# Another order of small constants and two paddings in SBUF under a two-layer float32r encoder kernel

## Chip, cores and metric

One NeuronCore of one Trainium2 chip runs the whole program. The metric is the device time of one execution in microseconds. Of the kernel before, three runs are shown: 2837.61, 2838.25 and 2838.52 us, median 2838.25 us.

## What is computed

Two encoder layers over 1024 tokens of 1024 channels, all in float32. Each layer is a token mixer, a SwiGLU FFN and a gated embedding, each with a norm ahead and a residual behind:

```python
for i in range(2):
    hn = rms_norm(h, norm_mix[i])
    mix = gla_mixer(hn, ...) if i == 0 else diff_attn_mixer(hn, ...)
    h = h + mix
    h = h + swiglu(rms_norm(h, norm_ffn[i]), ffn_w_in[i], ffn_w_out[i])   # hidden width 2816
    gate = sigmoid(rms_norm(h, ple_norm[i]) @ ple_w_gate[i])
    h = h + gate * (p[i] @ ple_w_proj[i])
```

The first mixer is a bidirectional gated linear attention of 4 heads, the second a differential softmax attention of 8 heads.

## The kernel before

**Products.** Every large product is split into high and low float32r parts and taken as three matmuls (`mm3`, L146 to L150). The first operand is the stationary one (loaded as weights), the second is streamed:

```python
def mm3(ps, lhs, rhs, start, stop):
    (lh, ll), (rh, rl) = lhs, rhs
    nc.tensor.matmul(ps, lh, rl, start=start, stop=False)   # L148
    nc.tensor.matmul(ps, ll, rh, start=False, stop=False)   # L149
    nc.tensor.matmul(ps, lh, rh, start=False, stop=stop)    # L150
```

So each matmul has its own weight load (LDWEIGHTS), and the weights of the next one are loaded while this one streams.

**Stages, in order of time.** GLA: projections in pieces of a few matmuls (`trans_proj`, `tok_proj`) strewn among the steps of the recurrence (`sps`, `ups`, `ops`, `kups`), then its output projection (`out_tiles`, names `go`). FFN of layer 0: input projection by Strassen-Winograd products (`prod`, L923; names `f_0ps` to `f_21ps`; 22 units of 7 products of 12 matmuls with 512 columns), then the output projection (`out_step`, L1017; `f0o`). The embedding's gate (`Ple.gate`, L1162; `pl`). The differential attention: values (`Values.blocks`, `dv`), then a pipeline of projections (`pmm`, `dp`), scores (`qkt`, `da..s`), transposes (`T`, `da..tp`; `tkm`, `dp..tk`) and value products (`AV`, `da..av`), its output projection (`do`); FFN and gate of layer 1 (`f1o`). The order on TensorE, VectorE, ScalarE and GpSimd is written out by hand and is not touched.

**Where tiles lie.** Pools opened on the left are stacked upward in SBUF in the order in which they are opened: `const`, `praw`, `pw`, `ph`, `tiny` (L80 to L84), then the stage's own pool (`gla`, `fx0`, `diff`, ...). Pools on the right (`hxg`, `hxd0`) are stacked downward from the top. Within a pool, tiles stand in the order in which their tags first appear; each is rounded up to 32 bytes a partition. The first free byte on the left is 16512, which is 128 modulo 512; the top is 480 modulo 512. Nearly all large tiles are multiples of 512 bytes, so a whole pool has one residue, shifted by the small tiles that stand before it:

| tiles (address modulo 512) | before |
|---|---|
| `ident`, `identr` (operands of transposes) | 128 |
| `praw`, `pw`, `ph`: FFN input weights, transposed tiles of `go`, `do` and gates, projection weights and values of the attention | 384 |
| left stage pools: FFN operands `T` 1, 2, 7, 6, gate weights, `kst`, `dq`, half of `hxd` | 256 |
| GLA's tiles behind `mid` (`qk`, `ku`, `vv`, `s`, `p`) | 128 |
| right pools: `hxg`, the other half of `hxd`, FFN operands `T` 5, 3, 4, output weights of layer 0 | 480 |

The pairs (streamed, weights) that follow: FFN input products (256, 384) and (480, 384), in both layers; `f0o` (480, 480) behind its first 48 matmuls, which have (384, 384); `f1o` in turns of 48 matmuls (256, 480) and (480, 480); `go` (480, 384); `do` half (480, 384) and half (256, 384); gates (256, 384); `dv` and `dp` (384, 480) and (384, 256); `AV` (256, 384); scores (256, 256); `ups`, `ops`, `sps` (128, 128).

Of the kernel before, what the change touches and what calls it, by code (L numbers as in the profile page):

```python
# [9 lines left out]
F32 = mybir.dt.float32  # L10
# [8 lines left out]
P = 128  # L19
# [15 lines left out]
PACE, PACE_END = 0.67, 0.72    # microseconds of projections among a step's stages  # L35
# [7 lines left out]
# what precedes the recurrence of the first mixer, in the order in which it is emitted  # L43
# [21 lines left out]
def kernel(  # L65
# [22 lines left out]

    ident = const.tile([P, P], F32, name="ident")
# [3 lines left out]
    mhalf = const.tile([P, 8], F32, name="mhalf")  # L93
# [34 lines left out]
    def block_t(pool, name, bufs=2):  # L128
        """16 KB: four rows of 1024."""
        return pool.tile([P, 4, D], F32R, tag="x", name=name, bufs=bufs)  # L130

    def load_wout(w, pools, bufs, name, engs, lead=1):
        """Output weights, k by k, in blocks that held the projections' operand."""
        wo, raw = [], {}
        for k in range(-1, KT):
            for i in range(0 if k < 0 else k + lead, min(k + lead + 1, KT)):
                raw[i] = rawt(f"{name}{i}_raw")
                nc.sync.dma_start(raw[i], w[sl(i), :])
            if k >= 0:
                if k % 4 == 0:  # L140
                    blk = [block_t(pools[k // 4], f"{name}{k}{z}", bufs) for z in range(2)]
                wo.append(both(blk, ALL, k % 4))
                hi_lo(raw.pop(k), *wo[k], engs[k % len(engs)])
            yield wo
# [53 lines left out]
    def load_p(layer, i, raw):  # L198
        """256 tokens of the embedding, channels on partitions."""
        nc.sync.dma_start(raw, p[layer, 0][:, sl(i, 256)].rearrange("(k p) t -> p k t", p=P))  # L200
# [12 lines left out]
    # ---------------------------------------------------------------- GLA  # L213
    def gla(hx, hx_pool, gain):
        """The mixer; returns the residual tiles, a per-tile generator and its pool."""
# [7 lines left out]
        # The gates' projections have 32 channels z between them. The first takes the weights' high parts three  # L223
        # times and the low parts side by side, so that two passes do (the fourth group of rows has the product
        # with the low parts); the second takes all its products in one pass, with the rows
        # (high, low, high, rest) of z over the rows (high, high, low, high) of its weights.
        wg = pool.tile([P, 2, 512], F32R, name="wg")
        bg = const.tile([P, 2, GH], F32, name="bg")
# [24 lines left out]
        rs = const.tile([P, GH, NT], F32, name="rs")  # L253
# [4 lines left out]
        # --- projections: generators that yield after every few products  # L258
        class W:
            """One weight block, loaded and split in parts of 4 KB."""  # L260
# [28 lines left out]
        def trans_proj(w, dst, key, nm):  # L289
            """Channels on partitions: [128, 1024]."""  # L290
            t = ht(nm + "T", [2, 512])
            dst[key] = t.rearrange("p a b -> p (a b)")
            ps = ptA(nm + "ps")
            for half in range(2):
                for k in range(KT):
                    mm3(ps[:, half, :], w.at(k), hx_k(hx, k, half), k == 0, k == KT - 1)
                    yield 0.65
            yield 0.0
            nc.scalar.copy(t, ps)

        def tok_proj(w, emit, nm):
            """Tokens on partitions: per token tile [128, 256]."""
# [13 lines left out]
        def ple_proj(w, nm):  # L316
            """The embeddings' projection, for later."""
# [51 lines left out]
        def jobs(names):  # L369
            """A chain of projections; the next weights are loaded and split one ahead."""  # L370
# [8 lines left out]
            for j, (n, h) in enumerate(names):  # L379
# [9 lines left out]
                if nxt:  # L389
                    nxt.load()  # L390
                    todo = list(nxt.parts())
                    # parts that must wait for this block's slots are split after it
                    free = 6 - 2 * len(list(w.parts())) if n + nxt.name[1] != "rp" else 4
                    early, todo = todo[:free // 2], todo[free // 2:]
                else:
                    early = []
# [18 lines left out]
        # --- log-gate sums of (head, direction): inclusive running sums, over a token tile (from its  # L415
        # far end for the backward direction), of TAU times the log gates; channels on partitions
# [25 lines left out]
        def gc(h, d, half):  # L442
            if (h, d) not in gate:
                gate[h, d] = (ht(f"B{h}_{d}"), pool.tile([P, 3, NT], F32, tag="mid", name=f"mid{h}_{d}", bufs=4))
# [19 lines left out]
        # --- the recurrence, by steps (head, direction, tile)  # L464
# [155 lines left out]
        # --- the first head's operands, by halves of the tokens  # L620
# [85 lines left out]
        # The steady state is a pipeline of one step; (stage, offset) in the order in which a step emits them.  # L706
        # F is a share of the projections; the gates of a head take the steps of the head before.
# [26 lines left out]
        # the output weights take the place of the projections' operand, half by half  # L734
# [49 lines left out]
    mid = {}    # what goes between the halves of an output tile  # L784

    def out_tiles(hs, h_dram, wo, load, comp, nm):
        """h += source @ wo, by token tiles; yields the tile that is done (or a negative number) and, between, None."""
# [29 lines left out]
    # ---------------------------------------------------------------- FFN  # L817
    # The input projection is taken in Winograd's form of Strassen's product: per pair of blocks of 128
    # channels (rows of A = W^T), K halves and token halves (columns of B; even and odd token tiles),
    # seven products in place of eight.  # L820
    #   products: 1 = A11 B11, 2 = A12 B21, 3 = S4 B22, 4 = A22 T4, 5 = S1 T1, 6 = S2 T2, 7 = S3 T3
    #   S1 = A21 + A22, S2 = S1 - A11, S3 = A11 - A21, S4 = A12 - S2
    #   T1 = B12 - B11, T2 = B22 - T1, T3 = B22 - B12, T4 = B21 - T2
    #   C11 = 1 + 2, C12 = 1 + 6 + 5 + 3, C21 = 1 + 6 + 7 + 4, C22 = 1 + 6 + 5 + 7
    def ffn(layer, hs, tiles, g, hx_pools, bufs, next_pool, early):
        """From the mixer's tiles on; returns the tiles of h after the FFN."""
# [9 lines left out]
        # --- operand B: norm, sums (in place, tokens on partitions), transposes  # L836
# [28 lines left out]
        def put_x(t):  # L865
            """Transposes of a tile; its halves, then what the sums make of them, are kept in its place."""
# [22 lines left out]
        # --- operand A: unit u has the channel blocks 2 (u // 2) and the next, of the gate or the up half  # L889
# [32 lines left out]
        # --- products and what they go into  # L922
# [7 lines left out]
        def evac(u, p):  # L930
# [5 lines left out]
            if u < 2 and p == 2:  # L936
                # here the second product comes before the sixth, which still needs the first
# [22 lines left out]
        # --- the order of the products on the tensor engine; for the first two units around the last transposes  # L960
# [9 lines left out]
        def prepare(n):  # L970
            """All that comes before the split of product n."""
# [13 lines left out]
        # --- the output projection, by halves of the tokens (four tiles) with all of K on chip  # L985
# [54 lines left out]
        with tc.manual_schedule(engines={E.PE, E.DVE, E.Activation, E.Pool}):  # L1040
            at = {"mul": 0, "put": 0}

            def advance(t, n):
                """What goes before output tile t (n = -1) and after its halves."""
# [28 lines left out]
            for z in seq:  # L1073
# [6 lines left out]
                else:  # L1080
# [9 lines left out]
                    # the second product is added when the first is no longer wanted  # L1090
                    # from the third unit on, the second product waits for the sixth
# [25 lines left out]
    # ---------------------------------------------------------------- per-layer embedding  # L1117
# [18 lines left out]
    class Ple:  # L1136
        """The gate and its sum into the residual, by token tiles; the next layer's norm follows where there is one."""
# [50 lines left out]
    # ---------------------------------------------------------------- differential attention  # L1188
    class Values:
        """Values of all heads, by blocks of 256 channels."""  # L1190
# [39 lines left out]
    def diff(hx, hx_pools, h_dram, val, between):  # L1230
# [12 lines left out]
        ls = const.tile([P, 2], F32, name="ls")  # L1243
        neglam = const.tile([P, 1], F32, name="neglam")
# [31 lines left out]
        # query and key weights of one head  # L1276
# [19 lines left out]
        # The steady state is a pipeline of period two query tiles. An attention step takes the  # L1296
        # query tile i of all heads, a projection step the token tile u, a value step the pair m.
# [50 lines left out]
        # the query tiles 2 m and 2 m + 1 together, channels on partitions  # L1348
# [133 lines left out]
        # (stage, offset) in the order in which a period emits them; pairs count in periods  # L1482
# [17 lines left out]
        def piece():  # L1500
            """A part of the values' projection; with it the weights of the first heads."""
# [44 lines left out]
        def ple_proj():  # L1546
            """The second layer's embeddings' projection, half a tile at a time."""
# [66 lines left out]
    # ---------------------------------------------------------------- the trunk  # L1614
# [97 lines left out]
_LAYOUT = {'p': (0, 1, 3, 2)}    # channels before tokens  # L1712
# [40 lines left out]
```

## Time and profile before

| | |
|---|---|
| median of 3 runs | 2838.25 us |
| profiled execution, span | 2836.8 us |
| TensorE busy | 2774.1 us, 98% of the span, 15272 matmuls |
| VectorE, ScalarE, GpSimd busy | 55%, 46%, 42% |
| bytes moved by DMA | 283.59 MB, mean 100 GB/s |
| granted TensorE clock, mean | 0.998 |

The page gives the span alone for the profiled execution; the median lies 1.4 us above it. A matmul's duration in the trace overlaps that of the next one, so durations do not add up; what adds up is the spacing from one matmul's start to the next one's.

### The profile page before, as it was taken

What the parts mean: (1) busy time and instruction counts of PE and PEld (TensorE: products, weight loads), DVE (VectorE), ACT (ScalarE), POOL (GpSimd) and SP (SyncE); (2) the same over time, 40 slices, a digit from 0 to 9 for tenths busy, and PEclk for the clock granted to TensorE, in tenths of its full rate; (3) what the DMA queues carried; (4) which work ended last, traced back from release to release, by engine and by line L of the source; (5) the groups of instructions that cost most, each with busy time, mean ns of one, the idle gap of its engine ahead of it and who ended that gap; (6) DMA issues with size and microseconds to landing.
All of it is one profiled execution on the core that took longest, in us unless ns stands there. A gap on an engine that the chain in (4) does not pass through costs nothing.

```text
span 2836.8 us, 40481 instructions
## 1 busy us (share of the span) xinstructions
PE 2774.1 (98%) x15272; PEld 2368.8 (84%) x15272; DVE 1565.1 (55%) x2390; ACT 1297.5 (46%) x2723; POOL 1203.4 (42%) x1364
## 2 busy tenths in 40 slices
PE   8999999999999999999999999989999999999999
PEld 7899988788888888889989999878878888888887
DVE  5677775644444434354169898884564444444333
ACT  5776673433322332233368788784342322342222
POOL 3233331455555420010588888872165555530000
PEclk9999999999999999999999999999999999999999
DMA  4121265122222564333211111135222222374422
GB/s 123 40 64 60 79 223 174 67 83 89 82 67 89 196 205 141 97 99 109 74 53 42 38 42 38 34 119 197 75 76 81 89 76 74 114 258 138 146 68 80
DMA packets 199955, 283.59 MB, mean 100 GB/s; under 512 B 14544, under 2 KB 158928, under 8 KB 199760
## 3 DMA queue, kind: packets, MB, share of 16 engines
q1 hardware_dynamic: 199760, 281.00, 30.7%
q8 instruction: 121, 1.98, 0.3%
q14 instruction: 74, 0.61, 0.1%
HBM read 215.95 MB, written 65.01 MB: 99 GB/s over the span
## 4 chain that ended last, share of the span: by engine, by line
PE 81%; DVE 8%; POOL 5%; ACT 3%; issue 2%; DMA 1%; SPq 0%; POOLq 0%; DVEq 0%; ACTq 0%
PE f1o L148 3%; PE f1o L150 3%; PE f1o L149 3%; PE f0o L148 3%; PE f0o L149 3%; PE f0o L150 3%; PE dp L148 1%; PE dp L150 1%; PE dp L149 1%; PE dv L148 1%; PE dv L150 1%; PE dv L149 1%; PE do L148 1%; PE do L149 1%; PE do L150 1%
## 5 line engine op out<-in xcount | busy, mean ns | idle before, releaser
L148 PE MATMUL dp<-dw,hxd 128*128 128x256 f32 x512 | 148.5, 290 | 2.0 <-DVE da5dt L1345 0.3
L150 PE MATMUL dp<-dw,hxd 128*128 128x256 f32 x512 | 144.1, 281 | 0.0
L149 PE MATMUL dp<-dw,hxd 128*128 128x256 f32 x512 | 143.9, 281 | 0.0
L148 PE MATMUL f1o<-f1W,f1A 128*128 128x512 f32 x336 | 132.2, 393 | 0.0
L150 PE MATMUL f1o<-f1W,f1A 128*128 128x512 f32 x336 | 131.9, 393 | 0.0
L149 PE MATMUL f1o<-f1W,f1A 128*128 128x512 f32 x336 | 131.7, 392 | 0.0
L148 PE MATMUL f0o<-f0W,f0A 128*128 128x512 f32 x336 | 130.8, 389 | 0.0
L150 PE MATMUL f0o<-f0W,f0A 128*128 128x512 f32 x336 | 130.7, 389 | 0.0
L149 PE MATMUL f0o<-f0W,f0A 128*128 128x512 f32 x336 | 130.7, 389 | 0.0
L148 PEld LDWEIGHTS dp<-dw,hxd 128*128 128x128 f32 x512 | 96.6, 189 | 3.5 <-DVE da5dt L1345 0.6
L149 PEld LDWEIGHTS dp<-dw,hxd 128*128 128x128 f32 x512 | 96.7, 189 | 0.1
L150 PEld LDWEIGHTS dp<-dw,hxd 128*128 128x128 f32 x512 | 96.5, 189 | 0.0
L150 PEld LDWEIGHTS f1o<-f1W,f1A 128*128 128x128 f32 x336 | 63.0, 188 | 14.6
L149 PEld LDWEIGHTS f1o<-f1W,f1A 128*128 128x128 f32 x336 | 63.0, 188 | 14.3
L148 PEld LDWEIGHTS f1o<-f1W,f1A 128*128 128x128 f32 x336 | 63.0, 188 | 14.3
L150 PEld LDWEIGHTS f0o<-f0W,f0A 128*128 128x128 f32 x336 | 63.1, 188 | 13.2
L148 PEld LDWEIGHTS f0o<-f0W,f0A 128*128 128x128 f32 x336 | 63.1, 188 | 13.1
L149 PEld LDWEIGHTS f0o<-f0W,f0A 128*128 128x128 f32 x336 | 63.1, 188 | 12.9
L148 PE MATMUL dv<-dwv,hxd 128*128 128x256 f32 x256 | 72.6, 284 | 0.0
L149 PE MATMUL dv<-dwv,hxd 128*128 128x256 f32 x256 | 71.9, 281 | 0.0
L150 PE MATMUL dv<-dwv,hxd 128*128 128x256 f32 x256 | 71.9, 281 | 0.0
L154 POOL TENSOR_SCALAR pn10r<-pn10ss 128x1 f32<-128x1 f32 x1 | 0.2, 191 | 169.1 <-ACT pn10xn L1146 169.1
(4446 smaller groups left out, 10022.0 us busy)
## 6 DMA issues: line engine op xcount, KB each, us to landing
pw_raw<-in_ple_w_gate_dram SPq DMA_DIRECT2D x16, 512.0 KB, 6.1
dqk_raw<-in_diff_w_in_dram SPq DMA_DIRECT2D x32, 256.0 KB, 3.9
x<-in_x_dram SPq DMA_DIRECT2D x8, 512.0 KB, 5.9
wv_raw<-in_gla_w_in_dram SPq DMA_DIRECT2D x8, 512.0 KB, 3.8
wr_raw<-in_gla_w_in_dram SPq DMA_DIRECT2D x8, 512.0 KB, 3.8
o_dram<-o SPq DMA_DIRECT2D x32, 128.0 KB, 1.9
r_dram<-r SPq DMA_DIRECT2D x16, 256.0 KB, 2.2
gwo_raw<-in_gla_w_out_dram SPq DMA_DIRECT2D x8, 512.0 KB, 3.7
```

The lines of the kernel that those rows point to most:

```text
L148: nc.tensor.matmul(ps, lh, rl, start=start, stop=False)
L149: nc.tensor.matmul(ps, ll, rh, start=False, stop=False)
L150: nc.tensor.matmul(ps, lh, rh, start=False, stop=stop)
L154: nc.gpsimd.tensor_scalar(r, ss, scale, EPS, ALU.mult, ALU.add)
```

## The change

Five small tiles of `const` (`mhalf`, `bg`, `rs`, `ls`, `neglam`) are allocated ahead of `ident`, with a padding of 96 bytes behind them, and `tiny` gets a padding of four buffers of 32 bytes. The tile `mid` grows from three rows to four (96 to 128 bytes a partition). Comments and docstrings are dropped too, which moves line numbers by up to four.

```diff
@@ tile_encoder_kernel, behind the pools
+    mhalf = const.tile([P, 8], F32, name="mhalf")
+    bg = const.tile([P, 2, GH], F32, name="bg")
+    rs = const.tile([P, GH, NT], F32, name="rs")
+    ls = const.tile([P, 2], F32, name="ls")
+    neglam = const.tile([P, 1], F32, name="neglam")
+    const.tile([P, 24], F32, name="pad0")
+    tiny.tile([P, 8], F32, tag="pad", name="pad1")
     ident = const.tile([P, P], F32, name="ident")
...
-    mhalf = const.tile([P, 8], F32, name="mhalf")
     nc.vector.memset(mhalf, -0.5)
@@ gla
-        bg = const.tile([P, 2, GH], F32, name="bg")
...
-        rs = const.tile([P, GH, NT], F32, name="rs")
...
-                gate[h, d] = (ht(f"B{h}_{d}"), pool.tile([P, 3, NT], F32, tag="mid", name=f"mid{h}_{d}", bufs=4))
+                gate[h, d] = (ht(f"B{h}_{d}"), pool.tile([P, 4, NT], F32, tag="mid", name=f"mid{h}_{d}", bufs=4))
@@ diff
-        ls = const.tile([P, 2], F32, name="ls")
-        neglam = const.tile([P, 1], F32, name="neglam")
```

The small tiles take 32 + 32 + 128 + 32 + 32 + 96 = 352 bytes, so `ident` starts at 16512 + 352 = 16864, which is 480 modulo 512; `identr` (512 bytes) and the 4 KB tile of the gains follow, and `praw` starts at 480 too. With the padding `tiny` ends at 480, and with four buffers of 128 bytes for `mid` all of GLA's later tiles do. Of the 15272 matmuls, 15144 then have (480, 480); the other 128 are transposes of keys in the attention, (480, 224). Before, 1584 matmuls of the FFN output projections have equal residues (`f0o` and half of `f1o`), and some 1200 short ones: the scores and GLA's small products.

The order of instructions is the same on every engine, and so are all waits; the only instructions that differ are the readers and writers of `mid`, whose row of 24 elements becomes one of 32.

## Rows read from the trace of the kernel before

**Rows 1.** The page: its head and the busy time of each engine.
```profile
span 2836.8 us, 40481 instructions
PE 2774.1 (98%) x15272; PEld 2368.8 (84%) x15272; DVE 1565.1 (55%) x2390; ACT 1297.5 (46%) x2723; POOL 1203.4 (42%) x1364
```
**Rows 2.** The page: the chain that ended last, shares of the span by engine.
```profile
PE 81%; DVE 8%; POOL 5%; ACT 3%; issue 2%; DMA 1%; SPq 0%; POOLq 0%; DVEq 0%; ACTq 0%
```
**Rows 3.** Stretches: length, busy of PE, PEld, DVE, ACT, POOL, clock, DMA, GB/s.
```profile
100.00:700.00 600.00, 583.29 (x3521) 511.18 (x3520) 380.90 (x772) 323.80 (x771) 231.01 (x220) 0.99 0.31 100
1280.00:1900.00 620.00, 598.67 (x4528) 556.10 (x4526) 454.05 (x658) 420.69 (x1036) 456.24 (x711) 1.00 0.19 58
```
**Rows 4.** Tile f0o: minimum/median/maximum duration in ns, first and last start in us.
```profile
L148 PE MATMUL f0o<-f0W,f0A x336: 387/389/482, 980.3 to 1209.1; 128*128 128x512 f32 x168
L150 PE MATMUL f0o<-f0W,f0A x336: 389/389/397, 980.8 to 1209.5; 128*128 128x512 f32 x168
L150 PE MATMUL f0o<-f_0wo,f_0ao x8: 387/389/389, 969.9 to 974.7; 128*128 128x512 f32 x8
```
**Rows 5.** Tile f1o, the same view of layer 1.
```profile
L148 PE MATMUL f1o<-f1W,f1A x336: 389/393/479, 2503.6 to 2736.2; 128*128 128x512 f32 x168
L150 PE MATMUL f1o<-f1W,f1A x336: 389/393/397, 2504.1 to 2736.7; 128*128 128x512 f32 x168
```
**Rows 6.** Tile f1o within 2548.3 to 2558.8 us, a turn with (256, 480).
```profile
L149 PE MATMUL f1o<-f1W,f1A x16: 393/394/397, 2548.1 to 2558.6; 128*128 128x512 f32 x16
```
**Rows 7.** Tile f1o within 2561.3 to 2569.8 us, a turn with (480, 480).
```profile
L150 PE MATMUL f1o<-f1W,f1A x14: 389/389/389, 2560.9 to 2569.8; 128*128 128x512 f32 x14
```
**Rows 8.** Stretches within f0o and the FFN input products, columns as in rows 3.
```profile
990.00:1080.00 90.00, 90.00 (x399) 74.55 (x398) 31.38 (x33) 32.31 (x40) 16.61 (x7) 1.00 0.61 198
720.00:820.00 100.00, 100.00 (x431) 80.79 (x430) 41.80 (x60) 28.48 (x49) 57.61 (x44) 1.00 0.26 84
2300.00:2400.00 100.00, 100.00 (x430) 80.46 (x429) 42.85 (x61) 31.22 (x55) 52.52 (x41) 1.00 0.25 81
```
**Rows 9.** Tiles go, do and pl03g: output projections and a gate.
```profile
L149 PE MATMUL go<-gwo,got x128: 388/394/402, 427.1 to 529.2; 128*128 128x512 f32 x128
L149 PE MATMUL do<-dwo,dot x128: 390/396/405, 1949.6 to 2051.6; 128*128 128x512 f32 x128
L149 PE MATMUL pl03g<-pg,pn x16: 390/392/404, 1247.8 to 1260.0; 128*128 128x512 f32 x16
```
**Rows 10.** PE in order of time: the first and the tenth matmul of f0o.
```profile
969.40 0.40 PE L148 MATMUL f0o<-f_0wo,f_0ao 128*128 128x512 f32 x1
...
971.48 0.39 PE L148 MATMUL f0o<-f_0wo,f_0ao 128*128 128x512 f32 x1
```
**Rows 11.** Tile da9s: the scores of one query tile, (256, 256).
```profile
L1303 PE MATMUL da9s<-kst,dq x8: 389/394/475, 1508.4 to 1513.6; 128*128 128x512 f32 x8
```
**Rows 12.** Stretches of 256-column matmuls alone (dv twice, then pl17g): PE, clock, DMA.
```profile
1325.00:1334.00 9.00, 9.00 (x78) 1.00 0.49 148
1406.00:1414.00 8.00, 8.00 (x70) 1.00 0.06 16
...
2827.00:2832.00 5.00, 5.00 (x44) 1.00 0.15 56
```
**Rows 13.** Tiles ups and dv: 256 columns, (128, 128) and (384, 480 or 256).
```profile
L149 PE MATMUL ups<-vv,ku x56: 274/281/415, 86.1 to 411.2; 128*128 128x256 f32 x56
L150 PE MATMUL dv<-dwv,hxd x256: 274/281/288, 1308.8 to 1432.3; 128*128 128x256 f32 x128
```
**Rows 14.** Tiles da9tp, da9ob and dp5tk: transposes with (128, 384), (128, 256) and (128, 0 or 256).
```profile
L1334 PE MATMUL da9tp<-ident,da9e x8: 272/273/331, 1523.3 to 1526.4; 128*128 128x128 f32 x8
L1365 PE MATMUL da9ob<-ident,da9oT x2: 271/272/272, 1621.6 to 1621.7; 128*128 128x128 f32 x2
L1452 PE MATMUL dp5tk<-identr,hl x4: 247/248/252, 1425.8 to 1426.1; 128*128 128x128 f32 x4
```

## Prediction

> **What bounds the kernel.** I read the page's head first: TensorE is busy for 2774.1 of 2836.8 us, the other engines for 42 to 55% [rows 1], and the chain that ended last lies on TensorE for 81% [rows 2]. By stretches, TensorE is without a gap in the FFN [rows 8] and idle for some 17 us in GLA's 600 us and some 21 us in the attention's 620 us [rows 3]. So time goes down only if TensorE's matmuls follow each other more closely. The change leaves every instruction, order and wait as it was; it can act through addresses alone. The question to the trace is then whether the spacing of matmuls depends on where their operands lie.
>
> It does, and the kernel before holds the comparison. `f0o` and `f1o` are the same 1008 matmuls of 512 columns, one per layer. In layer 0 both operands lie at 480 modulo 512, in layer 1 half of the matmuls stream from 256 against weights at 480. From the first start to the last, `f0o` takes 1209.5 - 980.3 = 229.2 us [rows 4] and `f1o` 2736.7 - 2503.6 = 233.1 us [rows 5]. Inside `f1o` the turns can be told apart: with (256, 480) each matmul lasts 393 to 397 ns, and 45 spacings take 10.5 us, 233.3 ns each [rows 6]; with (480, 480) minimum, median and maximum are 389 ns [rows 7]. In `f0o`, 399 matmuls touch a stretch of 90 us; the first of them may have begun 0.39 us earlier, so the spacing is 90.39 / 399 = 226.5 ns [rows 8]. The first 48 matmuls of `f0o`, with both operands at 384, reach the same 389 ns [rows 4]: it is the equality of the two that matters, not the value 480. By the same count the FFN's input products, with unequal residues, have 100.4 / 431 = 232.9 ns in layer 0 and 233.5 ns in layer 1 [rows 8]. The granted clock is 1.00 in all these stretches, the upper of its two levels (2.4 GHz), so it isn't the clock.
>
> One more row limits the gain. `f0o` begins behind products with unequal residues, and its first nine spacings take 971.48 - 969.40 = 2.08 us, 231 ns each [rows 10]; only then does it settle at 226.5. The scores have equal residues (256, 256) and still 394 ns [rows 11]: they come four at a time between other shapes and never settle. I take it that equal residues pay from about the tenth matmul of an unbroken run on, and not in short ones.
>
> **The change part by part.** Against the span of 2836.8 us:
>
> 1. *FFN input products.* 22 units x 7 products x 12 matmuls x 2 layers = 3696, all unequal now, all equal after. 232.9 to 233.5 less 226.5 is 6.4 to 7.0; I take 6.5: 24.0 us. Some 100 matmuls a layer at the start, broken by transposes and waits, don't settle: less 1.5. **-22.5 us.** Bound on the other side: 0, if the products don't settle at all, since here VectorE and ScalarE read PSUM between products while `f0o` holds its sums until the end.
> 2. *`f1o`.* It becomes what `f0o` is: 233.1 - 229.2. **-3.9 us.**
> 3. *`go`, `do` and the gates of 512 columns.* 384 + 384 + 744 matmuls, now 392 to 396 ns against 389 [rows 7, 9], about 5.5 ns more. They run in blocks of 48 between transposes, so 39 of 48 gain: 1512 x 0.8 x 5.5 = 6.7; **-6.7 us**, between -8 and -3.
> 4. *Other matmuls of 512 columns* (scores, GLA's q and k, the embeddings' projections, some 1130). Short runs: **0**, bounds -6 ns for the 620 that are unequal now (-3.7 us) and +2 ns for each (+2.3 us), the scatter between rows 9 and 11.
> 5. *Matmuls of 256 columns*: `dv` 768, `dp` 1536, `AV` 768, GLA's v and r 1536, `ups` and `ops` 432, 5040 in all. No long run of them with equal residues exists, so this is the open price. Now `dv` has 9.28 / 78 = 119.0 and 8.28 / 70 = 118.3 ns, the last gate 5.28 / 44 = 120.0 ns [rows 12]. Upper bound of the gain: settled, 512 columns take 226.5 ns, so 256 of them half, 113.3, which is 5.4 ns less than 118.7. It is supported by a difference: unequal, the second 256 columns of a matmul cost 232.9 - 118.7 = 114.2 ns, nearly the same, so the excess of 5 to 6 ns seems to belong to each matmul and not to its length. Lower bound: nothing, or even 120.0, the settled spacing of the last gate, 1.3 ns more. `ups` with (128, 128) has the same median of 281 ns as `dv` [rows 13], but it comes three at a time. I take the 5.4 ns as nearest to the difference just shown, for runs of 24 and more alone, from the tenth matmul on (0.6 of them): `dv` 768 x 0.6 x 5.4 = 2.5 us; `dp` and `AV` 2304 x 0.6 x 5.4 = 7.5 us, of which I count half, because the attention's 21 idle us [rows 3] show that its chains through VectorE and GpSimd (73 to 74% of that stretch each) also set the pace. GLA's short pieces: 0. **-6.2 us**, bounds -27 (5040 x 5.4) and +6.6 (x 1.3).
> 6. *Transposes*, 1400 or so: 272 to 273 ns with (128, 384) and 271 to 272 with (128, 256) [rows 14], so **0**; `dp..tk` spread over 247 to 252 [rows 14], 5 ns x 384 = 2 us either way.
> 7. *`mid`*: 328 instructions read or write rows of 32 elements in place of 24, with as many elements each. The paddings have no instruction. **0**; hidden behind TensorE, and 0 without that cover too, as the element counts stay.
>
> No step is moved past a queue and no wait is added. In the FFN the next resources are far off: VectorE 42%, GpSimd 58%, DMA 26% of the stretch [rows 8], so 2.8% less time for TensorE exposes none of them.
>
> Sum: -22.5 - 3.9 - 6.7 - 6.2 = -39.3; 2836.8 - 39.3 = 2797.5, and with the median's 1.4 us over the span **2799 us**.
>
> **The rivals.**
>
> *Only the output projections settle.* The input products change their weight tile every 12 matmuls, stream from another operand each time and share PSUM with the engines that read it. Then the first term is gone: 2799 + 22.5 = 2821 us. Against it: `f0o` changes its weights every matmul too and moves between tiles every 24, and within the FFN no gap in TensorE's work is left [rows 8].
>
> *Short runs settle too.* After the change nearly every matmul has one residue, so the state might survive a change of shape. Then terms 4 and 5 go to their bounds: -22.5 - 3.9 - 6.7 - 3.7 - 27 = -64, 2774 us. Against: the scores [rows 11] and `ups` [rows 13].
>
> *Nothing changes.* If the difference between `f0o` and `f1o` came from something else in layer 1, the time stays at 2838 us. Against it speak the turns within `f1o` [rows 6, 7]. The Trainium skill, in "TensorE: Matmul & The Clock Gate", Part 2 (What happens when you issue a matmul), says that the streamed operand and the weight load have two independent read ports, so that loading the next weights takes nothing from the running matmul; by it addresses can't matter and this rival would hold. The trace disagrees: 393 to 397 against 389 ns for the same matmul [rows 6, 7].
>
> *Slower.* The place is the long runs of 256 columns, 5040 matmuls. There a weight load falls due every 119 ns instead of every 230, and equal residues could settle on a worse spacing instead of a better one. The 512-column terms give 33.1 us, so it decides from 33.1 / 5040 = 6.6 ns more per matmul, 125.3 ns. At 128 ns it would be 9.3 x 5040 = 47 us, less 33: 2852 us. Against it: the longest of these `dv` lasts 7 ns over its median [rows 13], and an average there would be without example.
>
> **How the numbers follow.** The forecast as worked out has 0.74; only the output projections 0.10; short runs too 0.08; nothing 0.05; slower 0.03. The forecast's own range is the open prices: from -27 partly taken (some 20 us below 2799) to term 5 at +6.6 and term 3 at -3 (2799 + 6.2 + 6.6 + 3.7 = 2815). I let the range reach down to 2779 and up to 2822, which takes in the first rival and leaves out the other three, 0.16. A measurement of this kernel can tell about 0.2%, 5.7 us, from no change; the forecast and the first two rivals lie beyond it: faster 0.92, same 0.05, slower 0.03.
>
> **What would show it.** Right: the FFN's input products at a median of 389 ns and some 442 matmuls in 100 us in place of 431; `f1o` at 389 throughout and as long as `f0o`; `go`, `do` and gates at 389 behind their first nine; `dv` and `dp` below 281 ns in the later part of their runs. Wrong: input products still at 392 to 398 (the first rival); `dv` and `dp` at 285 and more (the last); TensorE's idle time in the attention grown by as much as its busy time fell (then half was still too much).

## The result and the profile after

The changed kernel takes **2805.51 us** (median of 4 runs, 2804.42 to 2806.3) against 2837.93 us (2836.2 to 2838.52) of the kernel before on the same chip: a ratio of 0.9884, interval [0.987, 0.9898]. That is 32.4 us less; the forecast was 2799, its range 2779 to 2822. The whole interval lies below 1 by more than the 0.2% that the prediction takes for the least that can be told: the kernel is faster. The profiled execution's span falls by 33.2 us, from 2836.8 to 2803.6.

The page's head and the shares of the chain that ended last, for the changed kernel, answer to [rows 1, 2]:

```profile
span 2803.6 us, 40481 instructions
PE 2742.5 (98%) x15272; PEld 2373.3 (85%) x15272; DVE 1571.3 (56%) x2390; ACT 1297.1 (46%) x2723; POOL 1204.1 (43%) x1364
...
PE 83%; DVE 7%; POOL 4%; ACT 3%; issue 2%; DMA 1%; SPq 0%; POOLq 0%; DVEq 0%; ACTq 0%
```

TensorE's busy time falls by 31.6 us with the same 15272 matmuls, and the other engines stay where they were to within 7 us. No other engine has become the bound.

Where it went shows in stretches of TensorE alone (length, busy, count, clock, DMA): one in each layer's FFN input products, then two in `dv`.

```profile
720.00:820.00 100.00, 100.00 (x442) 1.00 0.25 84
2280.00:2380.00 100.00, 100.00 (x442) 1.00 0.25 81
...
1310.00:1318.00 8.00, 8.00 (x69) 1.00 0.65 197
1380.00:1388.00 8.00, 8.00 (x69) 1.00 0.09 26
```

The input products now come 442 in 100 us where they came 431 and 430 [rows 8]: 100.39 / 442 = 227.1 ns in place of 232.9 and more. The `dv` matmuls of 256 columns have become slower, if by little: 8.28 / 69 = 120.0 ns, where [rows 12] gave 119.0 and 118.3.

The same by tiles of the changed kernel (minimum/median/maximum duration in ns, first and last start). L156 to L158 are the three matmuls of `mm3`, L148 to L150 before:

```profile
L156 PE MATMUL f_13ps<-f0T,f_13w x28: 389/389/389, 786.0 to 804.4; 128*128 128x512 f32 x28
...
L156 PE MATMUL f0o<-f0W,f0A x336: 389/389/476, 968.3 to 1197.0; 128*128 128x512 f32 x168
L158 PE MATMUL f0o<-f0W,f0A x336: 389/389/393, 968.7 to 1197.4; 128*128 128x512 f32 x168
...
L156 PE MATMUL f1o<-f1W,f1A x336: 389/389/481, 2476.1 to 2704.8; 128*128 128x512 f32 x168
L158 PE MATMUL f1o<-f1W,f1A x336: 389/389/397, 2476.6 to 2705.3; 128*128 128x512 f32 x168
...
L157 PE MATMUL go<-gwo,got x128: 387/389/396, 429.2 to 529.4; 128*128 128x512 f32 x128
L157 PE MATMUL do<-dwo,dot x128: 387/389/396, 1937.5 to 2037.3; 128*128 128x512 f32 x128
L157 PE MATMUL pl03g<-pg,pn x16: 389/389/395, 1235.0 to 1247.0; 128*128 128x512 f32 x16
L1307 PE MATMUL da9s<-kst,dq x8: 389/395/477, 1495.9 to 1501.1; 128*128 128x512 f32 x8
L156 PE MATMUL v1ps<-wv,hxg x64: 280/283/387, 106.6 to 138.9; 128*128 128x256 f32 x64
L158 PE MATMUL dv<-dwv,hxd x256: 278/283/286, 1294.8 to 1419.6; 128*128 128x256 f32 x128
```

Every long run of 512 columns has 389 ns as its median. The two output projections are equal now: `f0o` 1197.4 - 968.3 = 229.1 us, `f1o` 2705.3 - 2476.1 = 229.2, where they took 229.2 and 233.1 [rows 4, 5]. The scores keep 395 ns [rows 11: 394]. And the long runs of 256 columns have 283 ns: `dv` had 281 [rows 13], and GLA's values had 280 in the kernel before, of which this is one tile:

```profile
L148 PE MATMUL v1ps<-wv,hxg x64: 277/280/387, 106.2 to 138.2; 128*128 128x256 f32 x64
```

The first starts tell the same in order of time. `go` begins 2.1 us *later* than before (429.2 against 427.1 [rows 9]): GLA has lost. `pl03g` begins 12.8 us earlier (1235.0 against 1247.8), `do` 12.1 us (1937.5 against 1949.6): the attention between them has gained nothing. The last start of `f1o` is 31.4 us earlier (2705.3 against 2736.7 [rows 5]).

So the spacing from each start to the next one, summed by group over both traces, gives: all matmuls of 512 columns -39.2 us (input products 878.7 to 853.3), those of 256 columns **+5.3 us** (GLA's v and r +2.8, `dv` +1.0, `dp` +1.5), the 128-column ones and the waits around them +0.6. That is -33.4 us, and the span says -33.2. Two further profiled executions of the changed kernel (after_again and after_r5 below) give -37.7 and -35.9, +6.6 and +5.8, -0.8 and -1.2, so waits scatter by some 1 to 3 us in each group.

### The profile page after: what moved, and what is told of

It is laid out like the page before. It is cut to its first block, busy times and chain, and to the rows that moved or that the text cites. A ratio compares the mean times of both kernels' runs of the same rounds, so it can differ in the third digit from the quotient of the medians.

```text
span 2803.6 us, 40481 instructions
## 1 busy us (share of the span) xinstructions
PE 2742.5 (98%) x15272; PEld 2373.3 (85%) x15272; DVE 1571.3 (56%) x2390; ACT 1297.1 (46%) x2723; POOL 1204.1 (43%) x1364
## 4 chain that ended last, share of the span: by engine, by line
PE 83%; DVE 7%; POOL 4%; ACT 3%; issue 2%; DMA 1%; SPq 0%; POOLq 0%; DVEq 0%; ACTq 0%
PE f1o L158 3%; PE f0o L156 3%; PE f0o L157 3%; PE f1o L156 3%; PE f1o L157 3%; PE f0o L158 3%; PE dp L156 2%; PE dp L158 2%; PE dp L157 2%; PE dv L156 1%; PE dv L158 1%; PE dv L157 1%; PE do L158 1%; PE do L156 1%; PE do L157 1%
## 5 line engine op out<-in xcount | busy, mean ns | idle before, releaser
L156 PE MATMUL dp<-dw,hxd 128*128 128x256 f32 x512 | 149.0, 291 | 2.0 <-DVE da17dt L1349 0.3
L158 PE MATMUL dp<-dw,hxd 128*128 128x256 f32 x512 | 144.9, 283 | 0.0
L156 PE MATMUL f1o<-f1W,f1A 128*128 128x512 f32 x336 | 130.8, 389 | 0.0
L156 PE MATMUL f0o<-f0W,f0A 128*128 128x512 f32 x336 | 130.8, 389 | 0.0
L158 PE MATMUL f0o<-f0W,f0A 128*128 128x512 f32 x336 | 130.7, 389 | 0.0
L158 PE MATMUL f1o<-f1W,f1A 128*128 128x512 f32 x336 | 130.7, 389 | 0.0
L156 PEld LDWEIGHTS dp<-dw,hxd 128*128 128x128 f32 x512 | 98.1, 192 | 3.5 <-DVE da17dt L1349 0.6
L158 PEld LDWEIGHTS dp<-dw,hxd 128*128 128x128 f32 x512 | 97.9, 191 | 0.0
L158 PEld LDWEIGHTS f0o<-f0W,f0A 128*128 128x128 f32 x336 | 63.1, 188 | 13.2
L158 PEld LDWEIGHTS f1o<-f1W,f1A 128*128 128x128 f32 x336 | 63.1, 188 | 13.1
L156 PEld LDWEIGHTS f0o<-f0W,f0A 128*128 128x128 f32 x336 | 63.1, 188 | 13.1
L156 PEld LDWEIGHTS f1o<-f1W,f1A 128*128 128x128 f32 x336 | 63.1, 188 | 12.9
L156 PE MATMUL dv<-dwv,hxd 128*128 128x256 f32 x256 | 73.0, 285 | 0.0
L158 PE MATMUL dv<-dwv,hxd 128*128 128x256 f32 x256 | 72.4, 283 | 0.0
```

## The experiments

**The theories.** Mine: what counts is the difference between the two operands' addresses, and 256 columns settle at 120.0 ns where 512 settle at 226.7, so equality costs the shorter ones something. Rivals: the absolute address counts; the unit is 512 bytes, as the change assumes; the settled spacing goes up in fixed steps with length; the products gained by another tile's move; the 256-column loss comes from waits. The first two runs are bare matmuls, the others the whole kernel.

### m1_residues: bare matmuls at chosen differences

```python
def group(delta, cols, base=0, count=48):     # bytes, modulo 512
    for i in range(count):
        nc.tensor.matmul(ps[:, 0:cols], wt[:, w0 + (i % 8) * P:w0 + (i % 8 + 1) * P],
                         mv[:, m0 + (i % 8) * 512:m0 + (i % 8) * 512 + cols], ...)
```

> A bare row of matmuls in groups of 48, each with its own 128-column weights, sums into PSUM, and nothing else of the encoder (its output is zeros and the last group's sums). Groups of 512 and of 256 columns take weights whose address differs from the streamed operand's by 0, 32, ... 480 bytes modulo 512; then the length goes through 128 to 512 columns at difference 0; then both operands are moved together by 64, 256 and 480 bytes. In the changed kernel, with equal residues, 512 columns settle at 226.7 ns and 256 columns at 120.0 ns. Theory A, a fixed excess: settled, a matmul takes its columns at 2.4 GHz plus 13.3 ns whatever its length, so 256, 320, 384, 448, 512 columns take 120.0, 146.7, 173.3, 200.0, 226.7 ns, and 272 columns 126.7. Theory B, a grid: the spacing settles on multiples of 13.33 ns, so the same for these, but 264 and 272 columns take 120.0 or 133.3 ns and nothing between. Theory C, a share of the length (one part in 16): 320, 384, 448 take 141.7, 170.0, 198.3, and 256 is 113.3 unless the weight load holds it at 120. On addresses: if equality counts, 512 columns take 226.7 at difference 0 wherever both lie and 232 to 234 elsewhere; 256 columns take 120.0 at 0 and 117 to 120 elsewhere. If instead some other difference is better, a group falls below these.

Measured: the groups in order of time (start, length, the tile's name: `d` is the address of the weights minus that of the streamed operand, `c` the columns). A group's start to the next one's start is 48 spacings.

```profile
48.91 11.35 PE L102 MATMUL b0d32c512ps<-mv,wt 128*128 128x512 f32 x48
60.10 11.36 PE L102 MATMUL b0d64c512ps<-mv,wt 128*128 128x512 f32 x48
...
82.54 11.32 PE L102 MATMUL b0d128c512ps<-mv,wt 128*128 128x512 f32 x48
93.69 11.37 PE L102 MATMUL b0d160c512ps<-mv,wt 128*128 128x512 f32 x48
104.89 11.16 PE L102 MATMUL b0d192c512ps<-mv,wt 128*128 128x512 f32 x48
115.89 11.36 PE L102 MATMUL b0d224c512ps<-mv,wt 128*128 128x512 f32 x48
127.08 11.05 PE L102 MATMUL b0d256c512ps<-mv,wt 128*128 128x512 f32 x48
137.97 11.35 PE L102 MATMUL b0d288c512ps<-mv,wt 128*128 128x512 f32 x48
```

A difference of 32 gives (60.10 - 48.91) / 48 = 233.1 ns, 192 gives 229.2, and **256 gives 226.9**. The last 24 spacings of each group, where it has settled, are sharper: 226.67 ns at 0 and at 256; 228.9 at 192 and 448; 232.6 to 234.5 at every other multiple of 16 tried; 232.5 at 4 and 230.7 at 8. So the unit is 256 bytes, not 512. Three groups at equal addresses of 64, 256 and 480 bytes all settle at 226.7, so the absolute address doesn't count once the spacing has settled. A group at equal addresses that follows another length needs about nine spacings, 232 ns on average, before it settles; `f0o`, behind unequal products, needed as many [rows 10]. So does a group that follows one of the same length and the same difference when both operands have moved: by 64 bytes it took ten spacings, the first nine at 230.9 ns, and the two other moves took three and five. A second group at the same addresses is settled from its first matmul on, and so was the group at 256 behind the one at 224.

The same for 256 columns:

```profile
233.42 5.84 PE L102 MATMUL b0d32c256ps<-mv,wt 128*128 128x256 f32 x48
239.10 5.82 PE L102 MATMUL b0d64c256ps<-mv,wt 128*128 128x256 f32 x48
244.76 5.79 PE L102 MATMUL b0d96c256ps<-mv,wt 128*128 128x256 f32 x48
250.39 5.85 PE L102 MATMUL b0d128c256ps<-mv,wt 128*128 128x256 f32 x48
256.08 5.91 PE L102 MATMUL b0d160c256ps<-mv,wt 128*128 128x256 f32 x48
261.83 5.81 PE L102 MATMUL b0d192c256ps<-mv,wt 128*128 128x256 f32 x48
```

Here 96 is best, (250.39 - 244.76) / 48 = 117.3 ns; 128 has 118.5, 160 has 119.8. Settled: **120.0 at 0, 117.4 at 96, 118.8 at 128**. Equal addresses are among the worst places for 256 columns. And the lengths, at equal addresses:

```profile
318.61 5.47 PE L102 MATMUL b0d0c128ps<-mv,wt 128*128 128x128 f32 x48
323.92 5.55 PE L102 MATMUL b0d0c192ps<-mv,wt 128*128 128x192 f32 x48
329.31 5.94 PE L102 MATMUL b0d0c256ps<-mv,wt 128*128 128x256 f32 x48
335.08 7.20 PE L102 MATMUL b0d0c320ps<-mv,wt 128*128 128x320 f32 x48
342.12 8.48 PE L102 MATMUL b0d0c384ps<-mv,wt 128*128 128x384 f32 x48
350.44 10.08 PE L102 MATMUL b0d0c448ps<-mv,wt 128*128 128x448 f32 x48
360.36 11.09 PE L102 MATMUL b0d0c512ps<-mv,wt 128*128 128x512 f32 x48
```

Settled they are 111.7, 111.7, 120.0, 146.7, 173.3, 206.7 and 226.7 ns. From 256 to 512 columns 106.7 ns are added, 0.417 ns each, one cycle of the 2.4 GHz level. With 0.417 ns taken off for each column, 256, 320, 384 and 512 columns all leave 13.3 ns over. The five other lengths tried do not: 264 columns settle at 120.0 ns and leave 10.0, 272 at 125.2 (11.8), 288 at 131.7 (11.7), 448 at 206.7 (20.0), 496 at 223.3 (16.7). So the excess at equal addresses lies between 10 and 20 ns and is no share of the length. It is no fixed amount for all lengths either, and steps of 13.3 ns do not hold: none of the three theories of the expectation stands as it is. What stands is that 256 and 512 columns have the same excess. At 128 and 192 columns something else sets 111.7.

### m2_loads: is the excess the weight load's?

The same groups with 128, 96, 64 or 32 weight columns, and groups in which operands take turns between two addresses.

```diff
-            nc.tensor.matmul(ps[:, 0:cols], wt[:, w0 + (i % 8) * P:w0 + (i % 8 + 1) * P],
+            nc.tensor.matmul(ps[0:wcols, 0:cols], wt[:, w0 + (i % 8) * P:w0 + (i % 8) * P + wcols],
```

> Bare rows of 48 matmuls again, nothing of the encoder. First with weights of 128, 96, 64 and 32 columns, at difference 0 (eq) and 128 bytes (ne). If the settled excess of 13.3 ns is streaming time that the next weight load takes away, it falls with the load: 512 columns at difference 0 settle at 226.7, 223.3, 220.0, 216.7 ns and 256 columns at 120.0, 116.7, 113.3, 110.0; at difference 128 bytes the further excess of 6 ns falls too. If the excess belongs to the streaming alone, all four stay at 226.7 and at 120.0. 128 columns stay at 112 if the load of 128 weight columns sets the pace there, and fall with fewer. Then the streamed operand alternates between 0 and 96 bytes: in 'own' each matmul's weights lie where its own streamed operand does, in 'prev' where the streamed operand of the matmul before does, which streams while they are loaded. If the two meet because they read at the same time, 'prev' settles at 226.7 and 'own' stays at 231 to 234; if it is the matmul's own pair, the other way round. 'mvalt' (streamed at 0 and 256, weights at 0) is like difference 0 if 256 bytes is the period.

Groups in order of time (`eq` equal addresses, `ne` 128 bytes apart, `w` the weight columns):

```profile
26.30 11.04 PE L101 MATMUL eqc512w128ps<-mv,wt 128*128 128x512 f32 x48
37.19 11.21 PE L101 MATMUL eqc512w96ps<-mv,wt 128*96 128x512 f32 x48
48.23 11.20 PE L101 MATMUL eqc512w64ps<-mv,wt 128*64 128x512 f32 x48
...
81.53 11.04 PE L101 MATMUL nec512w96ps<-mv,wt 128*96 128x512 f32 x48
92.41 11.18 PE L101 MATMUL nec512w64ps<-mv,wt 128*64 128x512 f32 x48
...
125.81 5.61 PE L101 MATMUL eqc256w64ps<-mv,wt 128*64 128x256 f32 x48
131.26 5.60 PE L101 MATMUL eqc256w32ps<-mv,wt 128*32 128x256 f32 x48
```

For 256 columns the load matters: (131.26 - 125.81) / 48 = 113.5 ns with 64 weight columns, settled 113.3, in place of 120.0 with 128. For 512 columns a smaller load does not help: equal addresses take (37.19 - 26.30) / 48 = 226.9 ns with 128 weight columns and (48.23 - 37.19) / 48 = 230.0 with 96, and now it is 128 bytes apart that gives (92.41 - 81.53) / 48 = 226.7. So the excess is not simply proportional to the load, and the difference of addresses at which the spacing is short depends on the load's length. Matmuls of 128 columns at equal addresses settle at 111.7 ns with 128 weight columns, 85.0 with 96 and 60.0 with 64 and 32: down to 64 their pace is the load's.

Groups whose streamed operand takes turns between 0 and 96 bytes settle at neither 226.7 nor 234: 234.0 ns if each matmul's own weights take the same turns, 230.0 if the weights being loaded meanwhile, those of the next matmul, match the running stream. The second is nearer, but it doesn't reach 226.7. Groups in which only one of the two operands takes these turns, so that every other pair is equal, have 230.0 too. So "the load beside the stream must match it" is not the rule, or not the whole of it; that stays open. Turns between 0 and 256 bytes give 226.7, as they should with a unit of 256.

### e_no_pad0: without the first padding

```diff
-    const.tile([P, 24], F32, name="pad0")
```

The left pools go to 384 modulo 512, the right ones stay at 480. Of the FFN input products 2376 are equal (at 384), 1320 are not; `go`, half of `do` and half of `f1o` are not either.

> The changed kernel without the padding of 96 bytes in the pool of constants: every pool on the left falls from 480 to 384 modulo 512, the right pools stay at 480. 2376 of the 3696 FFN input matmuls then have (384, 384), 1320 have (480, 384); f1o is half unequal as in the kernel before; go and half of do are unequal; gates are (384, 384); half of dv and dp is (384, 480). If equality counts: 226.5 ns in the 2376, 233 in the others, so -16 us for the input products, -4 for the gates, -1 for do, +1 for half of dv and dp, and nothing for f1o: some -20 us against the kernel before, 2817 to 2819 us. If the value 480 counts, or the place of the pools: the (384, 384) products stay at 232 or more and the time at 2835 to 2838 us.

Measured: 2823.11 us, ratio 0.9948, interval [0.9931, 0.9965]; span 2821.7. So more than half of the change's gain is lost with 96 bytes. A stretch of the input products in layer 0, against 431 of before and 442 of after:

```profile
720.00:820.00 100.00, 100.00 (x436) 1.00 0.27 90
```

Products at (384, 384) gain, so it is equality and not the value 480. But they gain less than I expected, 12.2 us against the kernel before in place of 16. The reason is in the order of time, where equal products follow unequal ones:

```profile
752.34 0.40 PE L155 MATMUL f_11ps<-f0T,f_11w 128*128 128x512 f32 x1
...
754.41 0.39 PE L155 MATMUL f_11ps<-f0T,f_11w 128*128 128x512 f32 x1
...
758.50 0.39 PE L155 MATMUL f_11ps<-f0T,f_11w 128*128 128x512 f32 x1
```

The first nine spacings take 754.41 - 752.34 = 2.07 us, 230 ns each; the next eighteen 4.09 us, 227.2 each. At each change between unequal and equal products nine matmuls are spent on settling. Counted so (of runs of 48, 39 gain; of runs of 12, 3), some 1780 of the 2376 gain 6.5 ns, 11.6 us, near the 12.2 measured.

### e_mod256: equal modulo 256 only

```diff
-    const.tile([P, 24], F32, name="pad0")
+    const.tile([P, 88], F32, name="pad0")
```

To make room, `ident` becomes another view of `identr`. Left pools lie at 224 modulo 512, right pools at 480: differences of 256 in 1320 of the input products, in all of `go` and in half of `f1o`.

> The changed kernel with a padding larger by 256 bytes in the pool of constants, for which the transposes' two identity tiles become one: every pool on the left lies at 224 modulo 512, the right pools at 480, so operands are equal modulo 256 but not modulo 512 in 1320 of the FFN input products, in go, half of do and of f1o, and in half of dv and dp. If the period is 256 bytes, as the bare row showed (226.67 ns at difference 256): the same as the changed kernel, 2803 to 2808 us, FFN input products and f1o at 389 ns throughout. If it is 512: like the kernel without the padding, 2820 to 2824 us.

Measured: 2807.6 us (2803.65 to 2809.21), ratio 0.9891, interval [0.9876, 0.9906], against 2806.6 (2805.52 to 2809.82) and [0.9877, 0.9906] of the changed kernel in the same comparison (`after_again`):

> The changed kernel itself, on the same chip, to compare with: 2804 to 2807 us.

`f1o`, half of it at a difference of 256 (lines lie one further down in this kernel and in those that follow):

```profile
L158 PE MATMUL f1o<-f1W,f1A x336: 389/389/389, 2478.2 to 2706.9; 128*128 128x512 f32 x168
```

389 ns throughout: in the whole kernel too the unit is 256 bytes.

### e_shift96, shift96_r5 and e_shift96_all: 96 bytes for the 256-column products

The normed tokens are the weights of `dv`, `dp` and of GLA's v and r. They are put 96 bytes into tiles that are larger by 256, in GLA and for half of the attention's tokens (space does not allow more), with `ident` a view as above:

```diff
-        return tuple(pool.tile([P, KT, 512], F32R, tag="x", ...) for i in range(2))
+        wide = [pool.tile([P, KT * 512 + 64], F32R, tag="x", ...) for i in range(2)]
+        return tuple(z[:, 24:24 + KT * 512].rearrange("p (k t) -> p k t", t=512) for z in wide)
```

> The changed kernel (with one identity tile, to make room) in which the normed operand of the projections, the stationary one of dv, dp and GLA's v and r, starts 96 bytes into its buffer: in GLA everywhere, in the attention for the first half of the tokens. Everything else stays equal modulo 256. These matmuls of 256 columns then have the difference 96 that the bare row showed fastest (117.33 against 120.00 ns), GLA's q and k of 512 columns have 160 (233.3). If the residues cause it: dv and dp of the first half fall from 120.0 to some 117.5 ns, 1152 x 2.5 = 2.9 us; GLA's v and r get back the 2.8 us that they lost, q and k lose 1 us: 5 us less than the changed kernel, some 2800 us. If the 256-column matmuls are at 120 for another reason: 2805 to 2807 us, the loss of q and k.

Measured: 2803.23 us (2801.69 to 2804.49), ratio 0.9876, interval [0.9859, 0.9892]; beside the changed kernel's 2806.6 and its interval, which overlaps. That is 3.4 us less, where 5 had been expected. By groups, v and r take 2.9 us less, where 2.8 had been expected, but `dv` 0.9 less and `dp` 0.7 less, together 1.6 in place of 2.9; GLA's q and k, which stream the tokens and are now unequal, take 1.0 more. A second comparison was made to tell it from scatter, with one more kernel, in which *all* tokens of the attention are shifted by a small tile ahead of them. That kernel also shifts whatever uses these pools later:

```diff
+            pool.tile([P, 24], F32, tag="pre", ..., bufs=1)
             z = tuple(pool.tile([P, KT, 512], F32R, tag="x", ...) for i in range(2))
+            pool.tile([P, 40], F32, tag="post", ..., bufs=1)
```

> The kernel of e_shift96 again, beside the changed kernel on the same chip, to tell its 3.4 us from the scatter of runs. If the gain of the 256-column matmuls is real the median is 2 to 5 us below the changed kernel's; if it was scatter, within 1.5 us of it.

> The changed kernel beside shift96_r5, as in the runs before: a median of 2804 to 2808 us.

> Both halves of the normed tokens of the attention start 96 bytes into their pools, so that all of dv and dp (2304 matmuls of 256 columns) have their weights 96 bytes ahead of the streamed operand modulo 256, where e_shift96 had this for every other run of 24 or 48 alone. Other work that later uses the same two pools is shifted too: 792 FFN input products and do get 160, which the bare matmuls priced at 233.3 ns. If the runs of dv and dp that alternated between 96 and 0 lost their gain by settling anew, dv falls by 2 to 3 ns a matmul from the changed kernel's 120.7 and dp by 1.5 to 2.5 from 122.6 (2.5 to 6 us in all). If dp gains nothing again, its spacing is set by something else than addresses (its waits, or its change of shape). FFN products and do lose 792 x 6.5 + 384 x 5.5 = 7 us, so the total should be about 2806 to 2810 by the first, 2810 to 2813 by the second.

Measured: shift96_r5 2803.32 us (2802.27 to 2803.91), after_r5 2805.12 (2802.06 to 2807.44), e_shift96_all 2812.54 (2811.59 to 2813.49). Over these two comparisons, the shifted kernel has 8 runs with a mean of 2803.2, the changed one 8 with a mean of 2806.0: 2.9 us less, with an interval of about 1.9 us either way from their scatter. That is 0.1%: a gain, but less than one comparison alone can tell.

The middle matmul of `dp` by groups (busy us, mean ns), in the kernel before, after_r5, shift96_r5 and e_shift96_all:

```profile
L149 PE MATMUL dp<-dw,hxd 128*128 128x256 f32 x512 | 143.9, 281 | 0.0
```
```profile
L157 PE MATMUL dp<-dw,hxd 128*128 128x256 f32 x512 | 145.0, 283 | 0.0
```
```profile
L158 PE MATMUL dp<-dw,hxd 128*128 128x256 f32 x512 | 144.1, 281 | 0.0
```
```profile
L158 PE MATMUL dp<-dw,hxd 128*128 128x256 f32 x512 | 143.5, 280 | 0.0
```

Spacings of `dp`, each against the changed kernel in the same comparison: -0.7 us (e_shift96) and -1.8 (shift96_r5) with half of the tokens shifted, -3.0 with all. Part of that is scatter of waits. With the spacings of 132 ns and more left out, the `dp` matmuls at 96 bytes have 118.0 and 118.1 ns in the two runs of the half-shifted kernel and the equal ones beside them 119.7; with all shifted they have 118.1, and the changed kernel has 119.8. So a `dp` matmul at 96 bytes gains some 1.7 ns, whether its neighbours are shifted or not. Both theories of that expectation are out: turns between 96 and 0 do not cost the gain, and the spacing of `dp` does depend on addresses. e_shift96 showed -0.7 only because it spent 1.1 us more in waits than shift96_r5. Between the two shifted kernels nothing but addresses differs; against the changed one they also have one identity tile in place of two, but e_no_pad0, which keeps both, shows the same pair, 118.2 and 119.7.

`dv` has -0.9 with half and no more, -0.6, with all: its expected 2 to 3 ns a matmul were 0.8. Counted in the same way it has 117.5 ns in the shifted half of e_shift96 but 119.0 throughout e_shift96_all, at the same difference. So for 256 columns the difference alone does not fix the spacing; what else does stays open.

The total of e_shift96_all lies in the range that was given for the second theory, but not for its reason: 792 input products and `do` are at a difference of 160 in it. They cost 7.6 and 2.1 us, where 5.1 and 2.1 had been reckoned for the two. As in e_no_pad0, equal products settle anew behind unequal ones; 6.3 of the 7.6 us lie in spacings without a wait. Its layer 1 has the same kind of stretch as e_no_pad0:

```profile
2290.00:2390.00 100.00, 100.00 (x436) 1.00 0.23 74
```

## Why the prediction was right, and which step was not

*Spacing depends on where the two operands lie, and their equality counts.* Right for 512 columns, though the unit is 256 bytes, and the rival that nothing changes is out. For 256 columns the difference is not all: at the same residues, (384, 480), `dv` has 118.3 ns in the kernel before and 117.5 in e_no_pad0. The Trainium skill ("TensorE: Matmul & The Clock Gate", Part 2) says that a weight load takes no read bandwidth from the running matmul, as each has a read port of its own. By that the address could not matter; the bare matmuls disagree as the kernel does, with 226.7 or 233.3 ns for the same work at other addresses. How load and stream meet no run here shows.

*Term 1, input products, -22.5 us.* Measured -25.5. Of the 3696 spacings 3636 are under 250 ns in both traces; they fell by 6.36 ns each, 23.1 us, against the 6.5 taken, and the deduction of 1.5 us for the start of each layer was hardly needed. The other 2.3 us came in spacings with waits, and that part is luck of the execution: in after_r5 it is 0.6. The rival in which only the output projections settle is out: a change of weight tile or of streamed tile every 12 matmuls unsettles nothing as long as both stay at the same address modulo 256.

*Term 2, `f1o`, -3.9.* Measured -3.95. *Term 3, `go`, `do` and gates, -6.7.* Measured -2.0, -2.2 and -3.7: -7.8.

*Term 4, other runs of 512 columns, 0.* Measured -1.9, within the bounds; the scores moved by +0.1 (+1.0 and +1.1 in the two further executions).

*Term 5, 256 columns, -6.2.* **This step failed: measured +5.3.** It took the settled spacing to be "half" of 226.5, 113.3 ns, where it is 120.0. Bare matmuls show the same excess of 13.3 ns at 256 as at 512 columns when addresses are equal, so half the columns do not have half the excess; 113.3 came only with weight loads of 64 columns or fewer. The lower bound of the same step, "120.0, the settled spacing of the last gate, 1.3 ns more", was the right price, but by luck: that gate had unequal residues then, (256, 384), and its spacings came as 120, 123 and 117 ns in turn, where all are 120 now. The support I gave, that the second 256 columns cost 232.9 - 118.7 = 114.2 ns, subtracted two matmuls at unequal addresses, and at equal ones the second half costs 106.7. I had also not seen that GLA's v and r and half of `dv` and `dp` lay 96 bytes apart modulo 256 before, the best difference of those tried in the bare row, and the other half of `dv` and `dp` and all of `AV` 128 apart. By the bare prices the change costs 1536 x 2.6 + 2304 x 1.9 + 768 x 1.2 (`AV`) = 9.3 us; 5.3 came. The traces show two reasons. Before, these matmuls had 118.0 to 119.6 ns in the kernel where there was no wait, not 117.4 and 118.8. And now the first nine of each run take 118.7 to 119.4 ns, and only those from the tenth on 120.0.

*Terms 6 and 7, 0.* Right: transposes, `mid` and what waits around them add up to +0.6. No queue, engine or transfer took the place of what was saved.

*The rivals for short runs and for a loss* are both out: nothing that was short settled, and the 256-column spacing rose to 120.0, not to the 125.3 from which it would have decided.

The sum was -39.3 us and became -33.2. The 512-column terms came out 6.1 us larger than forecast (-39.2 for -33.1) and the 256-column term 11.5 us worse, so part of one error covered the other, which was luck.

## What to carry to other kernels

Where float32r matmuls of 512 columns with a weight load each run back to back, put streamed and stationary operands at the same address modulo 256, and keep both there over the whole run: it gave 6.4 ns in 233 per matmul here. Don't extend that to other lengths unmeasured; at 256 columns equality is among the slowest places (120.0 ns), and 96 bytes between the operands gave 117.4 to 119.0. A spacing is measured for each length, not scaled from another: at equal addresses four lengths from 256 to 512 left 13.3 ns over their columns, five others between 10.0 and 20.0.

## What the hardware showed that I had not expected

- The unit is 256 bytes: 226.67 ns at differences of 0 and 256, 228.9 at 192 and 448, 232.6 to 234.5 at the other multiples of 32.
- For 256 columns the order is another: in the bare row 117.4 ns at 96, 120.0 at 0 and 160. And the difference is not all: `dv` at 96 has 117.5, 118.3 or 119.0 ns in different kernels.
- With 96 in place of 128 weight columns the good and the bad place for 512 columns change sides: 230.0 at 0, 226.7 at 128.
- Matmuls of 128 columns take 111.7 ns with 128 weight columns and 60.0 with 64.
- After a change of difference or length, or when both operands move by 64 bytes, up to ten matmuls of 512 columns pass before 226.7 ns is reached.

Why the spacing is shorter at one difference than at another is not settled by these runs. That it depends on the difference of addresses, on the streamed length and on the load's length is shown.
